# A two-layer decoder trunk: stick-breaking scores ahead of the V projection, dilated values behind the next q and k

## The chip, the core and the metric

One core of a Trainium2 chip runs the whole kernel. The metric is device time in microseconds of one execution. The engines are PE (matrix products), DVE (vector work), ACT (activation functions and copies), POOL (a second, slower vector engine) and SP (which issues most transfers). Each engine works through its own instructions strictly in order and waits on semaphores for the others.

## The reference

The input is x of 1 x 512 x 1024, with two layers of weights. A layer is a half-weighted SwiGLU, a hybrid mixer and another half-weighted SwiGLU. The mixer is:

```python
proj = h @ w_in
q_d, k_d = rope(...), rope(...)              # 12 dilated heads in 3 groups
o_dil = sum over groups of softmax-denominator weight * dilated_window_attention
# stick-breaking, 4 heads:
log_keep = where(past, log_sigmoid(-z), 0)
after = reverse_cumsum(log_keep) - log_keep
w = where(past, exp(log_sigmoid(z) + after), 0);  o_sb = w @ v
y = sigmoid(gate_dil) * (o_dil @ w_proj_dil) + sigmoid(gate_sb) * (o_sb @ w_proj_sb)
return y @ w_out
```

All is in float32.

## The kernel before, in words

Activations lie transposed, as eight tiles of 128 features x 512 tokens. Each float32 operand is split into a high and a low part in a rounded format (fp32r), and each product is made of three matmuls: high x high, low x high, high x low (`mm3`, lines 142 to 144; `project` chains eight of these, 24 matmuls, into one PSUM bank). Weights come in one long stream from DRAM, packed in the order of use by `_pack_layer`; ACT makes their high part `whi` (line 76) and DVE the low part `wlo` (line 77), two quarters of a chunk ahead.

PSUM has eight banks in four tags of two: m, t, s and o. A new tile of a tag waits until whoever reads the old one is done.

The mixer works in stages. First the **V projection** in two halves of 512 columns, token-major: half 0 in banks m, m, t, t and half 1 in s, s, o, o, with 32 x 3 matmuls each (lines 328 to 330). After the first of eight k steps of half 0, `norm.finish()` makes the root mean square: `rt`, one number per token on partitions (line 212), and `rb`, the same broadcast over a tile (matmuls at line 215, ACT copy at line 218). The V halves are then split into high and low by `split_v`: ACT scales by `rt` into the high part (line 338), DVE subtracts (line 339). Half 0 gives v0 (dilated heads without regrouping) and vs (stick heads); half 1 gives v12, in 16 pieces of 32 partitions x 512, since it is regrouped by residue of the token.

Then, for each of two head pairs, `qk_pair("plain")` projects q and k into m banks and splits them (DVE reads them with `rb` at line 377), and `stick(p, qk)` computes two heads. For each head and each of four query tiles, with 128, 256, 384 and 512 keys, PE makes a score block in an s bank (lines 400, 401 and the mask at 435), ACT takes abs, exp and ln, DVE a max-add (line 442), a running sum (443) and a subtraction that frees the s bank (445), and ACT the final exp (446). The weights are then transposed on PE (line 455), split (409, 410), and multiplied by vs (459).

Then, for s = 0 and 1, the dilated heads: `dil_scores` projects three rope pairs of q and k (lines 372 to 375) and makes scores, `dil_softmax` the softmax over the groups, and `dil_values` the transposes (572, 589) and the products with v0 (581) and v12 (599). `split_o` gives od0 and od1 (`od1h` is written by ACT at line 422). Gate projections, which depend on nothing but the normed input, fill PE between these steps: the table `GATES` says which pair of gates is projected at which place. Last, gates are applied (line 638 on), y is formed, and the output projection adds into x.

The code is written in this order, and a scheduler with a model of the engines then interleaves it: each engine's order is fixed when the kernel is built.

Of the kernel before, what the change touches and what calls it, by code (L numbers as in the profile page):

```python
# [15 lines left out]
P = 128  # L16
# [89 lines left out]
def trunk(ctx, tc, xin, win, gains, rope, masks, out, depth):  # L106
# [14 lines left out]
    def bank(tag):  # L121
        return psum.tile([P, 512], F32, name="ps_" + tag, tag=tag)
# [12 lines left out]

    ident = const.tile([P, P], F32, name="ident")
    make_identity(nc, ident)
    ones = const.tile([P, P], F32, name="ones")
    nc.vector.memset(ones, 1.0)

    def mm3(ps, w, v, start, stop):
# [15 lines left out]
    class Norm:  # L157


        def __init__(self, g, table=None):  # L160
            self.g = g * KD
            self.table = table
            last = table is None
            self.last = last
            self.h = [None] * KD
            self.acc = None
            self.rest = []

# [108 lines left out]
    def mixer(norm, nxt):  # L277
# [38 lines left out]
        nc.scalar.dma_start(sr, rope[1])  # L316


        pv = []
        for half in range(2):  # L320
            pv.append([bank(b) for b in ("mmtt", "ssoo")[half]])
            for k in range(KD):
                wh, wl = weights.quarter()
                for j in range(NT):
                    c = slice(j * P, (j + 1) * P)
                    ps = pv[half][j]
                    a, b = h[k][0][:, c], h[k][1][:, c]
                    nc.tensor.matmul(ps, a, wh, start=k == 0, stop=False)
                    nc.tensor.matmul(ps, a, wl, start=False, stop=False)
                    nc.tensor.matmul(ps, b, wh, start=False, stop=k == KD - 1)  # L330
                if half == 0 and k == 0:
                    norm.finish()
                    nc.gpsimd.tensor_mul(cr, cr, norm.rb)
                    nc.gpsimd.tensor_mul(sr, sr, norm.rb)

            def split_v(dst, src, sc):
                v = src.rearrange("p (h d) -> p h d", d=HD)
                nc.scalar.activation(dst[:, :, 0, :], v, AF.Copy, bias=0.0, scale=sc)
                nc.vector.scalar_tensor_tensor(dst[:, :, 1, :], v, sc, dst[:, :, 0, :].bitcast(F32),
                                               ALU.mult, ALU.subtract)  # L340

            if half == 0:
                v0, vs = [], []
                for j in range(NT):
                    sc = norm.rt[:, j:j + 1]
                    for lst, nm, off in ((v0, "v0", 0), (vs, "vs", 256)):
                        t = vp.tile([P, 4, 2, HD], F32R, name=f"{nm}_{j}", tag=f"{nm}_{j}")
                        split_v(t, pv[0][j][:, off:off + 256], sc)
                        lst.append(t)
            else:  # L350
                v12 = vp.tile([P, 4, 8, 2, HD], F32R, name="v12", tag="v12")
                for j in range(NT):
                    for r in range(4):
                        src = slice(32 * r, 32 * r + 32)
                        split_v(v12[32 * j:32 * j + 32, r], pv[1][j][src], norm.rt[src, j:j + 1])

        def to_t(ap):
            return ap.rearrange("p (j m r) -> p j r m", j=NT, m=32, r=4)
# [4 lines left out]
        def qk_pair(kind, view_q, view_k):  # L363

            res = []
            for which in ("q", "k"):
                ps = bank("m")
                project(ps, h)
                a = work("qa")
                if kind == "rope":  # L370
                    b = work("qb")
                    nc.vector.tensor_mul(a, ps, cr)
                    nc.vector.stream_shuffle(b, ps, ROT)
                    nc.gpsimd.tensor_mul(b, b, sr)
                    nc.gpsimd.tensor_add(a, a, b)
                else:
                    nc.vector.scalar_tensor_tensor(a, ps, SC if which == "q" else 1.0, norm.rb,
                                                   ALU.mult, ALU.mult)
# [38 lines left out]
            nc.vector.tensor_add(of[own], po[0:64], of[own])  # L417

        def split_o(of, nm):
            hi = mp.tile([P, T], F32R, name=nm + "h", tag=nm + "h")  # L420
            lo = mp.tile([P, T], F32R, name=nm + "l", tag=nm + "l")
            nc.scalar.copy(hi, of)
            nc.vector.tensor_sub(lo, of, hi.bitcast(F32))
            return hi, lo

        def stick(p, qk):
            of = work("of")
            for e in range(2):
                hd = 2 * p + e
                ws = []  # L430
                for j in range(NT):
                    w = (j + 1) * P
                    z = bank("s")
                    scores(z[:, :w], qk[e], tile_c(j), slice(0, w), True, False)
                    nc.tensor.matmul(z[:, j * P:w], identr, msbr, start=False, stop=True, skip_group_check=True)
                    a = pp.tile([P, T], F32, name="sw", tag="pp")
                    c = wk.tile([P, T], F32, name="sc", tag="sc", bufs=2)
                    av, cv, zv = a[:, :w], c[:, :w], z[:, :w]
                    nc.scalar.activation(av, zv, AF.Abs, bias=0.0, scale=1.0)
                    nc.scalar.activation(av, av, AF.Exp, bias=0.0, scale=-1.0)  # L440
                    nc.scalar.activation(av, av, AF.Ln, bias=1.0, scale=1.0)
                    nc.vector.scalar_tensor_tensor(av, zv, 0.0, av, ALU.max, ALU.add)
                    nc.vector.tensor_tensor_scan(cv[:, ::-1], av[:, ::-1], ones[:, 0:1].to_broadcast([P, w]), 0.0,  # L443
                                                 ALU.add, ALU.mult)
                    nc.vector.tensor_sub(cv, zv, cv)
                    nc.scalar.activation(av.rearrange("p (j r m) -> p j m r", r=4, m=32),
                                         cv.rearrange("p (j m r) -> p j m r", r=4, m=32),
                                         AF.Exp, bias=0.0, scale=1.0)
                    ws.append(a)
                po = bank("o")  # L450
                for i in range(NT):
                    n = NT - i
# [11 lines left out]
        def gate(d, b):  # L464
# [3 lines left out]
            if 0 <= i < KD:  # L468
                g = xpool.tile([P, T], F32, name="gate", tag=f"x{i}")
            else:  # L470
                g = mp.tile([P, T], F32, name="gate", tag="gate", bufs=6)
            nc.vector.tensor_mul(g, ps, norm.rb)
            return g

# [3 lines left out]
            for d in GATES[s, g]:  # L478
                gates[d] = (gate(d, 0), gate(d, 1))

        def dil_scores(s, st_a, st_b, pn, pm):

            qk0 = qk_pair("rope", same, same)
            fill(s, 0)
            for e in range(2):
                for i in range(2):
# [124 lines left out]

        last_exp = [None]
        os_ = []
        qs0 = qk_pair("plain", same, to_t)
        os_.append(stick(0, qs0))
        qs1 = qk_pair("plain", same, to_t)
        os_.append(stick(1, qs1))
        od = []
        for s in range(2):
            tl = dil_tiles()  # L620
            dil_scores(s, *tl)
            dil_softmax(*tl)
            od.append(dil_values(s, tl[2], tl[3]))
            fill(s, 3)
        st.close()

        st = ExitStack()
# [108 lines left out]
def _pack_layer(a, l):  # L736
# [25 lines left out]
    mix = [kmajor([(v, 256), (vs, 256)]), kmajor([(v + 256, 512)])]  # L762
    for p in range(2):
        mix += [blk(qs + P * p), blk(ks + P * p)]
    for s in range(2):
        for g in range(4):
            if g < 3:
# [51 lines left out]
```

## Time and profile before

| | us |
|---|---|
| median of three runs | 2175.48 |
| their range | 2173.88 to 2178.55 |
| the profiled execution's own time | 2173.67 |
| its span in the trace | 2171.8 |
| PE busy | 2140.2 (99%) |
| DVE busy | 1190.5 (55%) |
| ACT busy | 890.4 (41%) |
| first mixer, V projection | 374.35 to about 419 |

The first mixer lies at about 372 to 728 us of the span. A row of a windows view gives the window, its length, then busy time and number of instructions of PE, PE's weight loads, DVE, ACT and POOL, then the granted PE clock (1.00 is full), the share of DMA and GB/s. A matmul's listed duration (0.39 us for 512 columns) overlaps the next one; the distance between starts (0.23 us) is what it takes. A row of a waits view reads "engine and line of the waiting instruction <- what ended the wait: us in total, times, the longest".

### The profile page before, as it was taken

To read this page: it belongs to the slowest core of one execution; us is meant where nothing else is said; L and a number is where in the kernel's file an instruction comes from. 1 tells how busy PE (TensorE), PEld (TensorE's weight loads), DVE (VectorE), ACT (ScalarE), POOL (GpSimd) and SP (SyncE) were. 2 spreads that over 40 slices of the span, in tenths; PEclk is the share of its full clock that TensorE was granted. 3 is DMA by queue.
4 is the path that set the end of the run, shared out by engine and by line. 5 is a ranking of instruction groups with operands and counts; after the bars stand their busy time and mean duration, and the time that the engine had idled before them with its cause. 6 is when DMAs were issued, how large, how long until landed. Compare 5 with 4: busy or idle time off the path is not lost.

```text
span 2171.8 us, 25973 instructions
## 1 busy us (share of the span) xinstructions
PE 2140.2 (99%) x9828; PEld 1766.4 (81%) x9828; DVE 1190.5 (55%) x1892; ACT 890.4 (41%) x1572; POOL 369.4 (17%) x392
## 2 busy tenths in 40 slices
PE   8999999999999999999999999999999999999998
PEld 7888888878887888888888888888788788888887
DVE  5444433589867544443344444336897765444433
ACT  5333323566464433333333333236564543333332
POOL 2222100021312122210022220000223212222100
PEclk9999999999999999999999999999999999999999
DMA  4333334232224333333233333333222243323322
GB/s 152 97 97 97 95 111 126 88 93 82 81 76 128 96 97 98 97 97 94 91 97 97 97 97 102 108 121 93 87 83 78 78 127 96 97 97 97 97 92 84
DMA packets 64622, 212.81 MB, mean 98 GB/s; under 512 B 7408, under 2 KB 9456, under 8 KB 64496
## 3 DMA queue, kind: packets, MB, share of 16 engines
q1 hardware_dynamic: 63920, 210.10, 31.0%
q8 instruction: 77, 1.26, 0.2%
q10 hardware_dynamic: 576, 1.05, 0.2%
q14 instruction: 49, 0.40, 0.1%
HBM read 200.63 MB, written 6.29 MB: 95 GB/s over the span
## 4 chain that ended last, share of the span: by engine, by line
PE 92%; DVE 4%; issue 1%; ACT 1%; POOL 1%; DMA 0%; SPq 0%; DVEq 0%; POOLq 0%; ACTq 0%
PE ps_o L142 14%; PE ps_o L143 14%; PE ps_o L144 14%; PE ps_m L142 9%; PE ps_m L143 9%; PE ps_m L144 9%; PE ps_t L142 5%; PE ps_t L143 5%; PE ps_t L144 5%; DVE wlo L77 1%; DVE sc L443 1%; PE ps_o L599 0%; PE ps_s L401 0%; PE ps_s L400 0%; DVE pt L560 0%
## 5 line engine op out<-in xcount | busy, mean ns | idle before, releaser
L77 DVE TENSOR_TENSOR wlo<-wraw,whi 128x512 fp32r<-128x512 f32 x736 | 597.7, 815 | 614.5 <-ACT whi L76 613.9
L76 ACT CAST whi<-wraw 128x512 fp32r<-128x512 f32 x736 | 454.4, 621 | 959.0 <-PE ps_o L143 488.1
L142 PE MATMUL ps_m<-xh,whi 128*128 128x512 f32 x992 | 390.7, 394 | 9.9 <-ACT whi L76 6.4
L144 PE MATMUL ps_m<-xh,wlo 128*128 128x512 f32 x992 | 390.3, 393 | 0.5 <-DVE wlo L77 0.5
L143 PE MATMUL ps_m<-xl,whi 128*128 128x512 f32 x992 | 390.3, 393 | 0.0
L142 PE MATMUL ps_o<-fh,whi 128*128 128x512 f32 (+1 forms) x748 | 285.8, 382 | 0.0
L143 PE MATMUL ps_o<-fl,whi 128*128 128x512 f32 (+1 forms) x748 | 285.7, 382 | 0.0
L144 PE MATMUL ps_o<-fh,wlo 128*128 128x512 f32 (+1 forms) x748 | 285.7, 382 | 0.0
L239 POOL TENSOR_TENSOR fg<-fg,fs 128x512 f32<-128x512 f32 x88 | 114.9, 1307 | 928.1 <-ACT fs L238 928.1
L142 PEld LDWEIGHTS ps_m<-xh,whi 128*128 128x128 f32 x992 | 187.3, 189 | 51.0 <-ACT whi L76 8.2
L144 PEld LDWEIGHTS ps_m<-xh,wlo 128*128 128x128 f32 x992 | 187.2, 189 | 39.8 <-DVE wlo L77 2.4
L143 PEld LDWEIGHTS ps_m<-xl,whi 128*128 128x128 f32 x992 | 187.4, 189 | 37.9 <-DVE xl L180 0.8
L142 PE MATMUL ps_t<-xh,whi 128*128 128x512 f32 x480 | 187.2, 390 | 0.0
L144 PE MATMUL ps_t<-xh,wlo 128*128 128x512 f32 x480 | 187.0, 390 | 0.0
L143 PE MATMUL ps_t<-xl,whi 128*128 128x512 f32 x480 | 187.0, 390 | 0.0
L142 PE MATMUL ps_o<-xh,whi 128*128 128x512 f32 x448 | 174.4, 389 | 0.0
L143 PE MATMUL ps_o<-xl,whi 128*128 128x512 f32 x448 | 174.4, 389 | 0.0
L144 PE MATMUL ps_o<-xh,wlo 128*128 128x512 f32 x448 | 174.4, 389 | 0.0
L142 PEld LDWEIGHTS ps_o<-fh,whi 128*128 128x128 f32 x748 | 140.5, 188 | 30.1
L144 PEld LDWEIGHTS ps_o<-fh,wlo 128*128 128x128 f32 x748 | 140.5, 188 | 30.1
L143 PEld LDWEIGHTS ps_o<-fl,whi 128*128 128x128 f32 x748 | 140.5, 188 | 30.0
L240 POOL TENSOR_TENSOR fg<-fg,rb 128x512 f32<-128x512 f32 x88 | 114.9, 1307 | 6.3
(205 smaller groups left out, 2684.5 us busy)
## 6 DMA issues: line engine op xcount, KB each, us to landing
wraw<-in_w_dram SPq DMA_DIRECT2D x367, 512.0 KB, 3.5
spill<-x SPq DMA_DIRECT2D x16, 256.0 KB, 2.1
kh<-kh SPq DMA_DIRECT2D x32, 128.0 KB, 3.0
x<-spill SPq DMA_DIRECT2D x16, 256.0 KB, 3.4
x<-in_x_dram SPq DMA_DIRECT2D x8, 256.0 KB, 5.5
out_dram<-o SPq DMA_DIRECT2D x8, 256.0 KB, 2.9
wraw<-in_w_dram SPq DMA_DIRECT2D x2, 256.0 KB, 4.2
cr<-in_rope_dram ACTq DMA_DIRECT2D x2, 256.0 KB, 2.8
```

The source lines that it names most:

```text
L76: nc.scalar.copy(hi, src)
L77: nc.vector.tensor_sub(lo, src, hi.bitcast(F32))
L142: nc.tensor.matmul(ps, w[0], v[0], start=start, stop=False, skip_group_check=True)
L143: nc.tensor.matmul(ps, w[0], v[1], start=False, stop=False, skip_group_check=True)
L144: nc.tensor.matmul(ps, w[1], v[0], start=False, stop=stop, skip_group_check=True)
L239: nc.gpsimd.tensor_mul(g, g, s)
L240: nc.gpsimd.tensor_mul(g, g, norm.rb)
L443: nc.vector.tensor_tensor_scan(cv[:, ::-1], av[:, ::-1], ones[:, 0:1].to_broadcast([P, w]), 0.0, ALU.add, ALU.mult)
```

## The change

The mixer's order is rewritten. q and k of both stick pairs come first, each with its scores (`stick_scores`, the first half of the former `stick`); `norm.finish()` moves behind the first q projection. Then come V's two halves (`project_v`), half 0 now in banks t, t, o, o and half 1 in m, m, t, t. Then `stick_values` for both pairs. `dil_values(0)` is held back until the q and k of s = 1 have been projected. Gates 2 and 3 are both projected at place (1, 0), and gate 7 joins 4, 5 and 6 at (1, 3). To make room, the score tiles of a head share buffers (`half`, `full`), `ones` shrinks, vs lies in another pool, and od0 and od1 reuse its buffers. The weights are packed in the new order. All products stay the same.

```diff
-GATES = {(0, 0): (), (0, 1): (0, 1), (0, 2): (), (0, 3): (2,), (1, 0): (3,), (1, 1): (), (1, 2): (), (1, 3): (4, 5, 6)}
+GATES = {(0, 0): (), (0, 1): (0, 1), (0, 2): (), (0, 3): (), (1, 0): (2, 3), (1, 1): (), (1, 2): (), (1, 3): (4, 5, 6, 7)}
+OTAGS = {"os0": ("os0h", "os0l"), "os1": ("os1h", "os1l"), "od0": ("vs_0", "vs_1"), "od1": ("vs_2", "vs_3")}
...
-        pp = pool(st, "mixp", 8)
+        pp = pool(st, "mixp", 10)
...
-            pv.append([bank(b) for b in ("mmtt", "ssoo")[half]])
+        def project_v(half):
+            pv = [bank(b) for b in ("ttoo", "mmtt")[half]]
...
-                if half == 0 and k == 0:
-                    norm.finish()
...
                 ps = bank("m")
                 project(ps, h)
+                if norm.rb is None:
+                    norm.finish()
...
-        qs0 = qk_pair("plain", same, to_t)
-        os_.append(stick(0, qs0))
-        qs1 = qk_pair("plain", same, to_t)
-        os_.append(stick(1, qs1))
+        sw = []
+        for p in range(2):
+            sw.append(stick_scores(qk_pair("plain", same, to_t)))
+        for half in range(2):
+            project_v(half)
+        for p in range(2):
+            os_.append(stick_values(p, sw[p]))
         od = []
+        held = None
         for s in range(2):
+            qk0 = qk_pair("rope", same, same)
+            if held:
+                od.append(dil_values(0, *held))
             tl = dil_tiles()
-            dil_scores(s, *tl)
+            dil_scores(s, qk0, *tl)
             dil_softmax(*tl)
-            od.append(dil_values(s, tl[2], tl[3]))
-            fill(s, 3)
+            held = tl[2], tl[3]
+        od.append(dil_values(1, *held))
+        fill(1, 3)
```

**First place: DVE behind the end of V's second half (layer 1).** A row reads: line, operation, what is written <- what is read, shape; the number behind a name tells buffers apart. Before, the splits of V's second half (v12, from the s and o banks) mix with weight splits:

```order
L339 SCALAR_TENSOR_TENSOR v12_3190<-ps_o_3053,rt_2889,v12_3190 32x8x64
L77 TENSOR_TENSOR wlo_3243<-wraw_3224,whi_3242 128x512
L339 SCALAR_TENSOR_TENSOR v12_3190<-ps_s_3051,rt_2889,v12_3190 32x8x64
L339 SCALAR_TENSOR_TENSOR v12_3190<-ps_o_3052,rt_2889,v12_3190 32x8x64
L339 SCALAR_TENSOR_TENSOR v12_3190<-ps_s_3050,rt_2889,v12_3190 32x8x64
L339 SCALAR_TENSOR_TENSOR v12_3190<-ps_o_3053,rt_2889,v12_3190 32x8x64
L77 TENSOR_TENSOR wlo_3270<-wraw_3267,whi_3269 128x512
L339 SCALAR_TENSOR_TENSOR v12_3190<-ps_s_3051,rt_2889,v12_3190 32x8x64
L377 SCALAR_TENSOR_TENSOR qa_3258<-ps_m_3223,rb_2904 128x512
L339 SCALAR_TENSOR_TENSOR v12_3190<-ps_o_3052,rt_2889,v12_3190 32x8x64
L339 SCALAR_TENSOR_TENSOR v12_3190<-ps_s_3050,rt_2889,v12_3190 32x8x64
```

After, they come from the m and t banks and mix with steps of the second stick pair, heads 2 and 3 (lines 447, 448 and 450 are the former 442, 443 and 445; 330 is the former 339, 81 the former 77). Nine rows stand between the first split and the rows below, the first split among them: five splits, head 2's last max-add, running sum and subtraction, each 128x512, and one weight split (wlo). Then comes head 3:

```order
L330 SCALAR_TENSOR_TENSOR v12_2861<-ps_m_3430,rt_2903,v12_2861 32x8x64
L330 SCALAR_TENSOR_TENSOR v12_2861<-ps_t_3431,rt_2903,v12_2861 32x8x64
L330 SCALAR_TENSOR_TENSOR v12_2861<-ps_t_3432,rt_2903,v12_2861 32x8x64
L447 SCALAR_TENSOR_TENSOR sw_3215<-ps_s_3217,sw_3215 128x128
L330 SCALAR_TENSOR_TENSOR v12_2861<-ps_m_3429,rt_2903,v12_2861 32x8x64
L330 SCALAR_TENSOR_TENSOR v12_2861<-ps_m_3430,rt_2903,v12_2861 32x8x64
L448 SCALAR_TENSOR_TENSOR sc_3221<-sw_3215,ones_109 128x128
L330 SCALAR_TENSOR_TENSOR v12_2861<-ps_t_3431,rt_2903,v12_2861 32x8x64
L330 SCALAR_TENSOR_TENSOR v12_2861<-ps_t_3432,rt_2903,v12_2861 32x8x64
L450 TENSOR_TENSOR sc_3221<-ps_s_3217,sc_3221 128x128
L447 SCALAR_TENSOR_TENSOR sw_3164<-ps_s_3229,sw_3164 128x256
L330 SCALAR_TENSOR_TENSOR v12_2861<-ps_m_3429,rt_2903,v12_2861 32x8x64
```

The last row is the fourth split of ps_m_3429, the one after which that bank is free; it is the thirteenth of the sixteen. The steps of heads 2 and 3 stand between the splits now, and no qa.

**Second place: PE at the end of V's second half (layer 1).** Before, V's last matmuls, into an o bank, are followed by the projection of the first stick q into an m bank:

```order
L330 MATMUL ps_o_3052<-whi_3140,xl7_2801 128x512
L328 MATMUL ps_o_3053<-whi_3140,xh7_2800 128x512
L329 MATMUL ps_o_3053<-wlo_3141,xh7_2800 128x512
L330 MATMUL ps_o_3053<-whi_3140,xl7_2801 128x512
L142 MATMUL ps_m_3223<-xh0_2086,whi_3158 128x512
L143 MATMUL ps_m_3223<-xl0_2087,whi_3158 128x512
L144 MATMUL ps_m_3223<-xh0_2086,wlo_3159 128x512
L142 MATMUL ps_m_3223<-xh1_2186,whi_3158 128x512
L143 MATMUL ps_m_3223<-xl1_2187,whi_3158 128x512
```

After, V's last matmuls go into a t bank, and score blocks of head 3 with 128, 256 and 384 keys follow (lines 402, 403 and 440 are the former 400, 401 and 435), then the first rope q projection into the m bank that ps_m_3429 had (line 146 is the former 142):

```order
L341 MATMUL ps_t_3432<-wlo_3520,xh7_2800 128x512
L342 MATMUL ps_t_3432<-whi_3519,xl7_2801 128x512
L402 MATMUL ps_s_3217<-kh_3160,qh_3116 128x128
L403 MATMUL ps_s_3217<-kl_2839,qh_3116 128x128
L440 MATMUL ps_s_3217<-msbr_150,identr_149 128x128
L402 MATMUL ps_s_3229<-kh_3160,qh_3116 128x256
L403 MATMUL ps_s_3229<-kl_2839,qh_3116 128x256
L440 MATMUL ps_s_3229<-msbr_150,identr_149 128x128
L402 MATMUL ps_s_3241<-kh_3160,qh_3116 128x384
L403 MATMUL ps_s_3241<-kl_2839,qh_3116 128x384
L440 MATMUL ps_s_3241<-msbr_150,identr_149 128x128
L146 MATMUL ps_m_3775<-xh0_2086,whi_3537 128x512
```

Projections that stood behind V now stand ahead of it, and a short run of score blocks separates V from the next projection.

**Third place: PE at the norm's broadcast (layer 1).** Before, the matmuls that broadcast rt (line 215) stand among V's:

```order
L330 MATMUL ps_t_2863<-whi_2926,xl4_2496 128x512
L328 MATMUL ps_t_2864<-whi_2926,xh4_2495 128x512
L329 MATMUL ps_t_2864<-wlo_2927,xh4_2495 128x512
L215 MATMUL ps_s_2899<-ident_104,rt_2889 128x128 x4
L330 MATMUL ps_t_2864<-whi_2926,xl4_2496 128x512
L328 MATMUL ps_m_2861<-whi_2942,xh5_2596 128x512
L329 MATMUL ps_m_2861<-wlo_2943,xh5_2596 128x512
```

After, they stand (line 220) between the projection of k of the first pair (ps_m_2930) and that of q of the second (ps_m_3076):

```order
L148 MATMUL ps_m_2930<-xh6_2701,wlo_2882 128x512
L146 MATMUL ps_m_2930<-xh7_2800,whi_2881 128x512
L147 MATMUL ps_m_2930<-xl7_2801,whi_2881 128x512
L148 MATMUL ps_m_2930<-xh7_2800,wlo_2882 128x512
L220 MATMUL ps_s_2913<-ident_104,rt_2903 128x128 x4
L146 MATMUL ps_m_3076<-xh0_2086,whi_2933 128x512
L147 MATMUL ps_m_3076<-xl0_2087,whi_2933 128x512
```

The broadcast moved from the middle of V to the border between two m-bank projections; the sum of squares (line 208 of the changed kernel) stands 14 matmuls ahead of it.

More of the change, by code (lines that the diff above doesn't have):

```diff
@@ L137, in trunk @@
     make_identity(nc, ident)
-    ones = const.tile([P, P], F32, name="ones")
+    ones = const.tile([P, 1], F32, name="ones")
     nc.vector.memset(ones, 1.0)
@@ L316, in mixer, with split_v @@
         nc.scalar.dma_start(sr, rope[1])
-        pv = []
-        for half in range(2):
-            pv.append([bank(b) for b in ("mmtt", "ssoo")[half]])
+        v0, vs = [], []
+        v12 = vp.tile([P, 4, 8, 2, HD], F32R, name="v12", tag="v12")
+        def split_v(dst, src, sc):
+            v = src.rearrange("p (h d) -> p h d", d=HD)
+            nc.scalar.activation(dst[:, :, 0, :], v, AF.Copy, bias=0.0, scale=sc)
+            nc.vector.scalar_tensor_tensor(dst[:, :, 1, :], v, sc, dst[:, :, 0, :].bitcast(F32),
+                                           ALU.mult, ALU.subtract)
+        def project_v(half):
+            pv = [bank(b) for b in ("ttoo", "mmtt")[half]]
             for k in range(KD):
@@ L325, in mixer @@
                     c = slice(j * P, (j + 1) * P)
-                    ps = pv[half][j]
                     a, b = h[k][0][:, c], h[k][1][:, c]
-                    nc.tensor.matmul(ps, a, wh, start=k == 0, stop=False)
-                    nc.tensor.matmul(ps, a, wl, start=False, stop=False)
-                    nc.tensor.matmul(ps, b, wh, start=False, stop=k == KD - 1)
-                if half == 0 and k == 0:
-                    norm.finish()
[L333 to L344, printed above, removed]
+                    nc.tensor.matmul(pv[j], a, wh, start=k == 0, stop=False)
+                    nc.tensor.matmul(pv[j], a, wl, start=False, stop=False)
+                    nc.tensor.matmul(pv[j], b, wh, start=False, stop=k == KD - 1)
+            for j in range(NT):
+                if half == 0:
                     sc = norm.rt[:, j:j + 1]
-                    for lst, nm, off in ((v0, "v0", 0), (vs, "vs", 256)):
-                        t = vp.tile([P, 4, 2, HD], F32R, name=f"{nm}_{j}", tag=f"{nm}_{j}")
-                        split_v(t, pv[0][j][:, off:off + 256], sc)
+                    for lst, nm, off, pl in ((v0, "v0", 0, vp), (vs, "vs", 256, mp)):
+                        t = pl.tile([P, 4, 2, HD], F32R, name=f"{nm}_{j}", tag=f"{nm}_{j}")
+                        split_v(t, pv[j][:, off:off + 256], sc)
                         lst.append(t)
-            else:
-                v12 = vp.tile([P, 4, 8, 2, HD], F32R, name="v12", tag="v12")
-                for j in range(NT):
+                else:
                     for r in range(4):
                         src = slice(32 * r, 32 * r + 32)
-                        split_v(v12[32 * j:32 * j + 32, r], pv[1][j][src], norm.rt[src, j:j + 1])
+                        split_v(v12[32 * j:32 * j + 32, r], pv[j][src], norm.rt[src, j:j + 1])
         def to_t(ap):
@@ L368, in qk_pair @@
                 project(ps, h)
+                if norm.rb is None:
+                    norm.finish()
+                    nc.gpsimd.tensor_mul(cr, cr, norm.rb)
+                    nc.gpsimd.tensor_mul(sr, sr, norm.rb)
                 a = work("qa")
@@ L424, in split_o, with stick_scores @@
             return hi, lo
-        def stick(p, qk):
-            of = work("of")
+        def stick_scores(qk):
+            half = pp.tile([P, T], F32, name="sw", tag="pp")
+            heads = []
             for e in range(2):
-                hd = 2 * p + e
+                full = [pp.tile([P, T], F32, name="sw", tag="pp") for _ in range(2)]
                 ws = []
@@ L449, in stick, with stick_values @@
                     ws.append(a)
+                heads.append(ws)
+            return heads
+        def stick_values(p, heads):
+            of = work("of")
+            for e, ws in enumerate(heads):
+                hd = 2 * p + e
                 po = bank("o")
@@ L470, in gate @@
             else:
-                g = mp.tile([P, T], F32, name="gate", tag="gate", bufs=6)
+                g = mp.tile([P, T], F32, name="gate", tag="gate", bufs=8)
             nc.vector.tensor_mul(g, ps, norm.rb)
```

28 lines of the change are left out of this document (15 added, 13 removed).

## The prediction

> **What bounds the kernel now.** I read the page first, then the stretches of the first mixer with their idle time, then the waits of PE, then the groups of one shape for durations. The page's engine line and the chain:
>
> ```profile
> PE 2140.2 (99%) x9828; PEld 1766.4 (81%) x9828; DVE 1190.5 (55%) x1892; ACT 890.4 (41%) x1572; POOL 369.4 (17%) x392
> PE 92%; DVE 4%; issue 1%; ACT 1%; POOL 1%; DMA 0%; SPq 0%; DVEq 0%; POOLq 0%; ACTq 0%
> ```
>
> TensorE (PE) is the bound. The change adds and removes no matmul, so it can only change how long PE waits, and how fast it runs. The stretches of the first mixer show where PE waits today; PE's busy time is the second number after the window's length.
>
> ```profile
> core 0: us, PE busy (x) PEld busy (x) DVE busy (x) ACT busy (x) POOL busy (x), PEclk, DMA share, GB/s
> 372.00:420.00 48.00, 48.00 (x221) 39.92 (x220) 19.81 (x35) 18.42 (x33) 5.07 (x6) 1.00 0.36 113
> 420.00:440.00 20.00, 20.00 (x89) 16.30 (x88) 19.24 (x27) 16.67 (x25) 0.00 (x0) 1.00 0.22 65
> 460.00:482.00 22.00, 17.38 (x87) 13.58 (x86) 18.90 (x29) 11.91 (x27) 6.11 (x4) 1.00 0.28 78
> 560.00:604.00 44.00, 42.45 (x228) 35.10 (x227) 37.27 (x84) 17.91 (x36) 19.12 (x38) 1.00 0.26 72
> 649.00:654.00 5.00, 3.70 (x18) 2.27 (x17) 2.11 (x4) 1.82 (x3) 0.00 (x0) 1.00 0.00 0
> ```
>
> 372 to 420 is the V projection: PE never waits. 420 to 440 holds the split of V's second half on DVE and ACT: both are nearly full, and PE, which has query and key projections to do, still never waits. PE waits at the end of the first stick pair (22.00 - 17.38 = 4.62 us), in the dilated values of s = 0 (1.55) and at the end of the dilated values of s = 1 (1.30). PE's waits in those places, summed over both layers:
>
> ```profile
> PE ps_s L400 <- DVE sc L445: 3.9, 4, 1.3
> PE ps_t L142 <- ACT od1h L422: 2.6, 2, 1.3
> PE ps_m L142 <- DVE gate L472: 2.5, 2, 1.2
> ```
>
> The second layer repeats them, with one thing more:
>
> ```profile
> 1535.00:1557.00 22.00, 17.65 (x82) 13.79 (x81) 18.88 (x29) 12.45 (x28) 5.40 (x4) 0.95 0.30 84
> 1550.00:1554.80 4.80, 2.94 (x19) 2.24 (x17) 3.90 (x8) 2.96 (x7) 0.00 (x0) 1.00 0.13 51
> 1554.80:1558.20 3.40, 2.98 (x7) 2.41 (x8) 3.34 (x7) 3.13 (x8) 0.26 (x1) 0.50 0.50 96
> ```
>
> After a stretch in which PE was busy 2.94 of 4.80 us, the granted clock is 0.50 for 3.4 us. Two pairs of neighbouring matmuls inside it and behind it give the price:
>
> ```profile
> 1556.66 0.63 PE L142 MATMUL ps_m<-xh,whi 128*128 128x512 f32 x1
> 1557.09 0.63 PE L143 MATMUL ps_m<-xl,whi 128*128 128x512 f32 x1
> 1558.54 0.40 PE L144 MATMUL ps_m<-xh,wlo 128*128 128x512 f32 x1
> 1558.77 0.39 PE L142 MATMUL ps_m<-xh,whi 128*128 128x512 f32 x1
> ```
>
> 0.43 us from start to start against 0.23. Seven matmuls there lost 7 x 0.20 = 1.4 us. So the same stall cost 4.62 us in layer 1 and 4.35 + 1.4 = 5.75 in layer 2.
>
> **What the change gives back.** The scores of both stick pairs now run among the projections of the second pair and of V, so the DVE crowd at 460 to 482 is spread out: -4.6 in layer 1, -5.75 in layer 2. Held back, the first dilated values come behind the next q and k: I take half of the 1.55, -0.8 (an estimate between 0 and -1.55). At od1, 21 projection matmuls now stand between the last v12 matmul and the first that needs od1h, where three stood: at 0.23 us that is 4.8 us of cover against a wait of 1.30: -1.3. Gate 7's two projections leave the tail for this; there the output projection's first 21 matmuls need only y0 to y6, so I cost that at nothing (up to 1 us if that cover fails, counted below). Sum: -6.7 in layer 1, -7.85 in layer 2.
>
> **What it takes: V's second half.** This is the large term. V is now projected last, its second half into banks m, m, t, t, and what PE does next (second place in the order above) are three score blocks and then the q projection of the dilated heads, which needs the first of those m banks. On DVE (first place) 13 of the 16 splits of V, head 2's last step and head 3's first ones stand ahead of the release of that bank. The durations of V's splits, and of the shapes between them:
>
> ```profile
> L338 ACT ACTIVATE v<-ps_s,rt x8: 679/682/683, 417.9 to 429.0; 32x512 fp32r<-32x512 f32 x8
> L339 DVE SCALAR_TENSOR_TENSOR v<-ps_s,rt,v x8: 737/744/756, 418.6 to 431.6; 32x512 fp32r<-32x512 f32 x8
> L339 DVE SCALAR_TENSOR_TENSOR v<-ps_o,rt,v x8: 742/748/759, 420.2 to 436.1; 32x512 fp32r<-32x512 f32 x8
> ```
>
> ```profile
> L77 DVE TENSOR_TENSOR wlo<-wraw,whi 128x512 fp32r<-128x512 f32 x108 | 86.5, 807 | 47.7 <-ACT whi L76 47.5
> L443 DVE TENSOR_TENSOR_SCAN sc<-sw,ones 128x512 f32<-128x512 f32 x4 | 8.1, 2034 | 0.0
> L442 DVE SCALAR_TENSOR_TENSOR sw<-ps_s,sw 128x512 f32<-128x512 f32 x4 | 2.7, 680 | 0.0
> L445 DVE TENSOR_TENSOR sc<-ps_s,sc 128x512 f32<-128x512 f32 x4 | 2.7, 674 | 0.0
> L443 DVE TENSOR_TENSOR_SCAN sc<-sw,ones 128x128 f32<-128x128 f32 x4 | 2.4, 604 | 0.1
> L442 DVE SCALAR_TENSOR_TENSOR sw<-ps_s,sw 128x256 f32<-128x256 f32 x4 | 1.7, 417 | 0.0
> L445 DVE TENSOR_TENSOR sc<-ps_s,sc 128x128 f32<-128x128 f32 x4 | 1.1, 280 | 0.0
> L442 DVE SCALAR_TENSOR_TENSOR sw<-ps_s,sw 128x128 f32<-128x128 f32 x4 | 1.1, 279 | 0.0
> ```
>
> From the first split to the one that frees the bank: 13 x 0.747 = 9.7; head 2's 512-wide step 0.68 + 2.03 + 0.67; one wlo 0.81; head 3's 128-wide step 0.28 + 0.60 + 0.28; the start of the 256-wide step 0.42. The second group is 5.8, together 15.5 us. ACT makes the high part of each split in 0.68 and keeps ahead. DVE's first split began at 418.6 and V's last three matmuls were issued from
>
> ```profile
> 418.40 0.39 PE L328 MATMUL ps_o<-whi,xh 128*128 128x512 f32 x1
> ```
>
> on, 0.23 apart, to 419.1: DVE has a start of 0.5 us. PE has three score blocks in between: 128, 256 and 384 columns, twice each, and three masks of 128, 2 x 768 + 384 = 1920 columns at 0.23 / 512 each, about 0.9 us. Idle: 15.5 - 0.5 - 0.9 = 14.1; I take 14.0. PE meets it as two waits for a score bank (each for DVE's subtraction, about 5.9 and 7.9 us) and a rest of under 1 us for the m bank. Bounds: 8.6, if all of that but the splits were done earlier or lay under PE's work (9.7 - 1.1), and 15.5, if nothing overlaps.
>
> **The clock behind that wait.** 14 us of waiting with under 1 us of work in them is more than the 1.86 us in 4.80 that brought the clock to 0.50 in layer 2. I take +1.4 per layer once, with bounds of 0 (layer 1's 4.62 us of waits cost nothing, its row reads 1.00) and 2.8 (a drop in each of two places). The Trainium skill, TensorE: Matmul & The Clock Gate, section "What's actually happening", has a rule that speaks against this change: after one idle window of about 3.4 us the array gets half of its clock pulses, until it has been busy for about as long. By that rule the first matmuls after such a wait would lose about half of 3.4, 1.7 us as an estimate from that page; layer 2's rows, 3.4 us at 0.50, agree with it.
>
> **The first q and k.** Before, the norm's broadcast (rb) was made among V's matmuls, which don't need it (third place). Now q's and k's banks are the two m banks, and q1's projection must wait until DVE has read q0's with rb.
>
> ```profile
> 382.07 0.95 PE L203 MATMUL ps_s<-ones,acc 128*128 128x1 f32 x8
> 384.09 0.16 DVE L212 SCALAR_TENSOR_TENSOR rt<-ra,r 128x4 f32<-128x4 f32 x1
> L218 ACT COPY rb<-ps_s 128x512 f32<-128x512 f32 x1 | 0.6, 587 | 2.7 <-PE ps_s L215 2.7
> L377 DVE SCALAR_TENSOR_TENSOR qa<-ps_m,rb 128x512 f32<-128x512 f32 x4 | 2.8, 690 | 0.1
> ```
>
> rt is there 2.2 us after the sum of squares began, and in the changed order 14 matmuls (14 x 0.23 = 3.2 us) stand between the two: in time. Then 0.59 + 0.69 and the hand-overs, about 1.5 us, in PE's path (bounds 0.7 and 2.0).
>
> **Smaller waits.** PE changes kind more often (scores between V's matmuls), heads 1 and 2 may wait for a score bank, and the last k's DMA lands just ahead of the dilated scores. No row shows these in the new places; the nearest are the score waits above, 1.3 us at the longest. I take +1.0 per layer, bounds 0 and 3.0 (two such waits and the tail).
>
> **The sum.** Layer 1: 14.0 + 1.4 + 1.5 + 1.0 - 6.7 = +11.2. Layer 2: 14.0 + 1.4 + 1.5 + 1.0 - 7.85 = +10.05. Together +21.2. The profiled execution took 2173.67 us (its span is 2171.8), the median of the runs 2175.48, 0.1% more. 2173.67 + 21.2 = 2194.9; forecast 2195.
>
> **The rivals.**
>
> *Faster: the split stays hidden.* One mechanism: V's banks come free as fast as PE needs them. The row 420 to 440 speaks for it: 16 splits, PE at 20.00 of 20.00. But there PE had q and k projections for free m banks, 89 matmuls of cover; now nothing but 0.9 us of scores. The gains then stand against 1.5 + 1.0: -4.2 and -5.35, 2164. It decides where wait and clock together stay below 4.2 us per layer. Chance 0.11.
>
> *Half the wait.* DVE is through with head 2's 512-wide step when V ends, or PE reaches that place later than DVE does: the wait is 7 to 9 us. With 8.0: +5.2 and +4.05, 2183 (2179 to 2187). For it: the bound 8.6. Against it: the order of DVE is fixed and has the scan of 2.03 between the splits. Chance 0.20. Between this and the rival before lies no change, 2169.3 to 2178: 0.07, where gains and wait cancel.
>
> *The clock does not fall.* 2195 - 2.8 = 2192; layer 1's row of 1.00 speaks for it, layer 2's 0.50 against. It lies inside the forecast's own range. That the change does not do what it says (that the V projection is put back ahead of the scores in the program's order) is excluded by the rows in the order; I give it nothing.
>
> **How the numbers follow.** Forecast 0.62, with its own range of 2187 to 2207: the upper end is 15.5 + 2.8 + 2.0 + 3.0 - 6.7 = 16.6 in layer 1 and 15.45 in layer 2, together 32, or 2206. Range: from 2179, the lower end of the half wait, to 2207; it leaves out the faster rival and no change, 0.18, and little above. About 0.2% (4.35 us) is what a measurement of this kernel can tell from no change: faster 0.11, same 0.07, slower 0.62 + 0.20 = 0.82.
>
> **What would show it.** In the profile after: no wait in the first pair's last head (the 4.62 gone); no wait of PE for od1h; behind V's last matmul PE idle 12 to 15 us per layer, put down to DVE's score subtraction (line 450 of the changed kernel) and to a split of V (its line 330); a granted clock below 1.00 right after; PE idle about 1.5 us behind the broadcast of rb. I am wrong if PE works on through V's split, or if a third place waits as long as that one.

## The result and the profile after

The changed kernel takes 2186.43 us (2186.26 to 2186.89, 4 runs) against 2174.78 for the kernel before (4 runs): ratio 1.0053, 95% interval 1.0041 to 1.0065, 11.65 us slower. The forecast was 2195, range 2179 to 2207: direction and main cause right, the size nearly twice too large. The two profiled executions are 13.2 us apart (2186.89 and 2173.67), their spans 13.3 (2185.1 and 2171.8); what follows accounts for these.

The page of the changed kernel: PE's work is the same, the span is longer.

```profile
span 2185.1 us, 26025 instructions
PE 2140.3 (98%) x9828; PEld 1771.1 (81%) x9828; DVE 1184.3 (54%) x1892; ACT 892.5 (41%) x1572; POOL 371.5 (17%) x392
```

The stretches of its first mixer; V's projection ends at 448.8:

```profile
core 0: us, PE busy (x) PEld busy (x) DVE busy (x) ACT busy (x) POOL busy (x), PEclk, DMA share, GB/s
372.00:390.00 18.00, 16.60 (x82) 13.76 (x81) 8.68 (x17) 7.77 (x14) 4.00 (x6) 1.00 0.43 142
446.00:464.00 18.00, 6.05 (x24) 4.88 (x24) 17.27 (x27) 17.26 (x30) 0.00 (x0) 0.69 0.13 42
464.00:487.00 23.00, 23.00 (x109) 19.12 (x109) 20.00 (x29) 13.41 (x25) 6.26 (x4) 0.95 0.14 47
560.00:604.00 44.00, 44.00 (x244) 38.03 (x243) 34.47 (x84) 21.93 (x50) 15.20 (x34) 1.00 0.25 78
```

One stretch stands out: 446 to 464 has PE at 6.05 of 18 us, with DVE and ACT nearly full and the clock below 1. Layer 2 has the same stretch, with nearly the same numbers, at 1527 to 1545:

```profile
1527.00:1545.00 18.00, 6.05 (x24) 4.91 (x23) 17.27 (x27) 17.26 (x30) 0.00 (x0) 0.72 0.15 46
```

The stretches with waits of before are clean (560 to 604 has 44.00 of 44.00). PE's largest wait, both layers together, and a selection of PE's rows behind V's end in layer 1 (start, listed duration; in brackets the idle time and its releaser):

```profile
PE ps_s L402 <- DVE sc L450: 23.7, 4, 7.1
```

```profile
448.54 0.40 PE L342 MATMUL ps_t<-whi,xl 128*128 128x512 f32 x1
448.95 0.28 PE L440 MATMUL ps_s<-msbr,identr 128*128 128x128 f32 x1
453.94 0.55 PE L402 MATMUL ps_s<-kh,qh 128*128 128x256 f32 x1 [4.71 <-DVE sc L450]
461.95 0.69 PE L402 MATMUL ps_s<-kh,qh 128*128 128x384 f32 x1 [7.14 <-DVE sc L450]
463.16 0.77 PE L146 MATMUL ps_m<-xh,whi 128*128 128x512 f32 x1
465.86 0.63 PE L146 MATMUL ps_m<-xh,whi 128*128 128x512 f32 x1
466.28 0.50 PE L147 MATMUL ps_m<-xl,whi 128*128 128x512 f32 x1
```

These are V's last matmul, rows of three score blocks with two long waits between them, then the q projection, whose first matmuls are 0.43 us apart instead of 0.23. On DVE, a selection of what PE waited for, from V's first split to the step that released the second score bank, and the split behind it that frees the m bank:

```profile
448.17 0.73 DVE L330 SCALAR_TENSOR_TENSOR v<-ps_m,rt,v 32x512 fp32r<-32x512 f32 x1
450.30 1.23 DVE L448 TENSOR_TENSOR_SCAN sc<-sw,ones 128x512 f32<-128x512 f32 x1
453.10 0.69 DVE L450 TENSOR_TENSOR sc<-ps_s,sc 128x512 f32<-128x512 f32 x1
...
461.60 0.29 DVE L450 TENSOR_TENSOR sc<-ps_s,sc 128x128 f32<-128x128 f32 x1
462.26 1.54 DVE L330 SCALAR_TENSOR_TENSOR v<-ps_m,rt,v 32x512 fp32r<-32x512 f32 x2
```

**An account from start to start.** A matmul of 512 columns is listed with 0.39 us but takes 0.23 in a full row, so idle time in a listing is too small by up to 0.16 for each wait. Two rows of the kernel before show it:

```profile
464.25 0.39 PE L142 MATMUL ps_m<-xh,whi 128*128 128x512 f32 x1
465.96 0.36 PE L400 MATMUL ps_s<-kh,qh 128*128 128x256 f32 x1 [1.32 <-DVE sc L445]
```

The starts are 1.71 apart, so 1.48 us were lost, not 1.32. So I took, for each PE matmul of the mixer, the distance to the next start less 0.2275, 0.171, 0.114 or 0.061 us (512, 384, 256, and 128 or fewer columns), and added up, place by place, what is left where it exceeds 0.12. Layer 1, in us (both kernels have 1636 matmuls there):

| place | before | after |
|---|---|---|
| behind the norm's broadcast | 0 | 1.62 |
| behind V's end: waits | 0 | 13.4 |
| matmuls at half clock after it | 0 | 1.5 |
| end of the first stick pair (464 to 482) | 5.54 | 0 |
| first dilated values (580 to 604) | 2.94 | 0 |
| a gate (627) | 0.64 | 0 |
| od1 (650) | 1.80 | 0 |
| others | 0.13 | 2.14 |
| all that are at most 0.12 over | 18.4 | 17.8 |
| sum | 29.4 | 36.4 |

The mixer took 345.0 us before and 352.0 after, and 346.0 and 352.3 in layer 2: +7.0 and +6.3.

### The profile page after: what moved, and what is told of

It is laid out like the page before. It is cut to its first block, busy times and chain, and to the rows that moved or that the text cites. A ratio compares the mean times of both kernels' runs of the same rounds, so it can differ in the third digit from the quotient of the medians.

```text
span 2185.1 us, 26025 instructions
## 1 busy us (share of the span) xinstructions
PE 2140.3 (98%) x9828; PEld 1771.1 (81%) x9828; DVE 1184.3 (54%) x1892; ACT 892.5 (41%) x1572; POOL 371.5 (17%) x392
## 4 chain that ended last, share of the span: by engine, by line
PE 96%; DVE 2%; ACT 1%; DMA 0%; POOL 0%; issue 0%; SPq 0%; DVEq 0%; ACTq 0%; POOLq 0%
PE ps_o L146 14%; PE ps_o L147 14%; PE ps_o L148 14%; PE ps_m L146 11%; PE ps_m L147 11%; PE ps_m L148 10%; PE ps_t L146 5%; PE ps_t L148 5%; PE ps_t L147 5%; PE ps_s L402 1%; PE ps_s L403 1%; PE ps_o L610 1%; PE ps_t L341 1%; PE ps_t L342 1%; PE ps_t L340 1%; DVE v L330 0%
```

## The experiments

The theory: PE waits behind V because the banks that it needs next (first for scores, then for the projection) are released in DVE's order behind V's splits; cure either the bank or the amount of work, and the wait goes. The rival: DVE has too much work in that stretch in all, and the wait moves on. A second question is which part of the change brought the gains. There are three sets of four kernels; the kernel before took 2173.95, 2174.59 and 2175.05 us beside them. A ratio is always to the kernel before of the same set.

**1. V's halves in the other order** (banks by position).

```diff
-        for half in range(2):
+        for half in (1, 0):
             project_v(half)
```

> The half of V with 16 small splits is projected first, the other half last; banks stay by position (t, t, o, o, then m, m, t, t). Theory (PE waits for banks that DVE frees in order behind V's splits): behind V's end stand 16 pieces of 0.48 us instead of 0.75, and fewer of them ahead of the m bank; PE waits about 5 us there in place of 13.4 and the clock stays up: 2186.4 - 2 x (14.9 - 5) = 2166.6 us, between 2162 and 2171. Rival (DVE has too much work in all, wherever the banks are): the wait moves, 2180 us or more.

2177.54 us (2174.94 to 2178.39), ratio 1.0016 [1.0007, 1.0026]. Faster than the changed kernel by 8.9 us, less than the theory's 19.8. Most of the wait moved to where the next half takes over the t banks (layer 1; behind V's end 1.7 us are left, in layer 2 4.2):

```profile
429.00:440.00 11.00, 6.92 (x24) 5.26 (x23) 9.16 (x14) 9.43 (x15) 0.00 (x0) 0.84 0.11 42
446.00:464.00 18.00, 16.50 (x81) 13.71 (x80) 14.38 (x29) 14.05 (x32) 0.00 (x0) 1.00 0.27 87
```

```profile
PE ps_t L340 <- DVE v L330: 4.1, 1, 4.1
```

The splits delay whichever matmul needs their bank next; here that was V's own second half. I had only thought of the m banks.

**2. V's banks**, the half with 16 splits in o and t.

```diff
-            pv = [bank(b) for b in ("ttoo", "mmtt")[half]]
+            pv = [bank(b) for b in ("mmtt", "oott")[half]]
```

> Only the banks of V are changed: first half in m, m, t, t, second half in o, o, t, t, so that both m banks are free at V's end. Theory (the bank, not the work, makes PE wait): the q projection follows V at once, 48 matmuls of cover for the splits; 13 to 14.9 us per layer go: 2186.4 - 2 x 13.9 = 2158.6 us, between 2156 and 2164, faster than before. Rival (too much DVE work in that stretch): PE waits as long a little later, 2183 to 2187 us.

2170.22 us (2169.51 to 2170.82), ratio 0.9982 [0.9973, 0.9991]: 16 us faster than the changed kernel and faster than before, by changing one string. The choice of banks is shown to make the wait. The string also changes PE's order: in the changed kernel PE met the wait at score blocks, which stood ahead of the projection; here, with its bank free, the projection starts straight behind V's last matmul and the first score block comes ten matmuls later.

```profile
448.58 0.39 PE L342 MATMUL ps_t<-whi,xl 128*128 128x512 f32 x1
448.81 0.39 PE L146 MATMUL ps_m<-xh,whi 128*128 128x512 f32 x1
451.08 0.23 PE L402 MATMUL ps_s<-kh,qh 128*128 128x128 f32 x1
```

But the theory's 2158.6 was missed: of the 27.8 us that it expected, 11.6 did not come, and waits stand 17 and 26 us behind V's end (the row of waits counts layer 1).

```profile
448.00:464.00 16.00, 16.00 (x75) 13.33 (x74) 15.40 (x23) 15.45 (x27) 2.92 (x2) 1.00 0.19 67
464.00:480.00 16.00, 12.01 (x51) 9.14 (x50) 15.53 (x23) 9.28 (x18) 5.59 (x4) 0.93 0.26 82
```

```profile
PE ps_m L146 <- DVE qb L375: 3.8, 2, 2.2
```

DVE is busy 15.4 and 15.5 of 16 us: 16 splits, head 3's steps and the weight splits are more than PE's cover there. Now the m banks are late because their readers (qa, qb) stand in the same queue. Theory and rival are each half right.

**3. V ahead of the scores again**, in its former banks and with the norm's broadcast among its matmuls, all else as changed (the banks, the broadcast and the packing are left out here).

```diff
+        for half in range(2):
+            project_v(half)
         for p in range(2):
             sw.append(stick_scores(qk_pair("plain", same, to_t)))
-        for half in range(2):
-            project_v(half)
```

> V is projected first again, in its former banks, with the norm's broadcast among its matmuls; scores of both pairs, then values, dilated values held back and gate 7 early stay as changed. Theory: neither the wait behind V (14.9 us with the clock) nor that for the broadcast (1.6) is there; of the 11 us of waits per layer that went, those at the end of the first pair may come back (5.5 us): between 2174.8 - 2 x 9.5 = 2155.8 and 2167 us. Rival (the gains hang on V standing behind the scores): 2172 to 2176 us.

2180.13 us (2178.28 to 2184.04), ratio 1.003 [1.002, 1.004]. My expectation fell, and so did the rival's. The wait at the end of the first pair is back, and a second one stands at the second pair; the stretch of the first dilated values has none:

```profile
460.00:482.00 22.00, 17.49 (x87) 13.70 (x87) 18.88 (x29) 11.92 (x28) 6.11 (x4) 1.00 0.25 79
518.00:532.00 14.00, 9.39 (x40) 6.73 (x39) 11.98 (x29) 10.94 (x22) 1.92 (x2) 0.88 0.31 95
560.00:604.00 44.00, 44.00 (x244) 37.99 (x243) 33.66 (x83) 20.54 (x49) 19.59 (x40) 1.00 0.22 70
```

So the gain at 464 to 482 belongs to V standing behind the scores, as the forecast had it.

**4. The tail alone on the kernel before**: dilated values held back, gates as changed.

> The kernel before with the tail parts alone: first dilated values held back behind the next q and k, gates as changed, vs and od sharing buffers. Theory: the waits in the first dilated values (about 2.9 us per layer, start to start) and at od1 (1.5) and one for a gate (0.5) go, about 0.8 come at the gates: 2174.8 - 2 x 4 = 2166.8 us, between 2164 and 2170. Rival (these waits went because the scores stand elsewhere): 2173 to 2177 us.

2177.25 us (2174.01 to 2179.65), ratio 1.0014 [1.0005, 1.0023]: slower, where I expected 7 us faster. The largest loss is at 520 to 532, first the kernel before, then this one:

```profile
520.00:532.00 12.00, 12.00 (x65) 10.27 (x64) 11.85 (x24) 7.88 (x15) 2.91 (x2) 1.00 0.24 66
```

```profile
520.00:532.00 12.00, 9.67 (x43) 7.65 (x42) 11.18 (x24) 6.34 (x12) 2.90 (x2) 0.86 0.23 66
```

**5. Fewer splits in the changed kernel.** Its banks stay; V's second half is split in 8 full-height pieces and regrouped by DMA.

```diff
-                        split_v(v12[32 * j:32 * j + 32, r], pv[j][src], norm.rt[src, j:j + 1])
+                    for g in range(2):
+                        t = xpool.tile([P, 4, 2, HD], F32R, name="vt", tag=f"x{2 * j + g}")
+                        split_v(t, pv[j][:, 256 * g:256 * g + 256], norm.rt[:, j:j + 1])
+                        for r in range(4):
+                            nc.sync.dma_start(v12[32 * j:32 * j + 32, r, 4 * g:4 * g + 4].bitcast(F32),
+                                              t[32 * r:32 * r + 32].bitcast(F32))
```

> The changed kernel, its banks as they are, but V's second half is split in 8 pieces of 128x256 (about 0.48 us on each of DVE and ACT) into the free x tiles and regrouped by 32 small DMAs, in place of 16 pieces of 0.75. Theory (PE waits for what stands in DVE's order ahead of the release of the m bank): 4 pieces and head 2's step, 1.9 + 1.9 = 3.8 us, stand there in place of 14.9; the clock stays up: 2186.4 - 2 x 11 = 2164 us, between 2161 and 2170. Rival (the DMAs on SP's queue hold up the weights, or PE waits for something else there): 2178 us or more.

2170.99 us (2168.42 to 2171.55), ratio 0.998 [0.9971, 0.9989]; 1 us over the theory's upper end (five small waits, 2.9 us together, stand at 472 to 478). The wait behind V is one of 2.45 us, with the clock at 1.00:

```profile
449.28 0.27 PE L443 MATMUL ps_s<-msbr,identr 128*128 128x128 f32 x1
452.00 0.47 PE L146 MATMUL ps_m<-xh,whi 128*128 128x512 f32 x1 [2.45 <-DVE vt L330]
452.31 0.40 PE L147 MATMUL ps_m<-xl,whi 128*128 128x512 f32 x1
```

Here the bank is the same and the work is less; in run 2 the work is the same and the bank another. Each alone takes 15 to 16 us off. So the wait is shown from both sides to come from what stands ahead of a bank's release.

**6. The second pair's q and k into o banks**, on top of run 2.

```diff
-                ps = bank("m")
+                ps = bank("o" if kind == "plain" and pairs[0] == 1 else "m")
```

> The variant with V's second half in o, o, t, t, and the second stick pair's q and k projected into o banks. Theory: the wait of 1.6 us per layer behind the norm's broadcast, put down to the m bank of q0, goes: 2170.2 - 2 x 1.6 = 2167.0 us. Rival: PE waits for the broadcast's readers all the same, 2170 us.

2166.90 us (2166.42 to 2167.23), ratio 0.9965 [0.9953, 0.9978]; 2167.0 was expected. The wait behind the broadcast (16.60 of 18 us in the changed kernel) is gone:

```profile
372.00:390.00 18.00, 18.00 (x84) 14.96 (x83) 6.75 (x14) 6.94 (x11) 2.08 (x4) 1.00 0.44 138
```

**7 and 8. Other banks and regrouping by DMA together**, with run 6's edit and without it.

> The last variant with V's second half regrouped by DMA as well. Theory: both remaining waits of the variant with other banks go, those behind V (1.8 + 2.4 and smaller, with 1.5 of half clock: 6 us per layer, from a DVE that is busy 15.5 of 16 us) and the 1.6: 2170.2 - 2 x 7.6 = 2155 us, between 2153 and 2160. Rival (DVE's crowd stays, since the steps of the stick heads fill it): 2165 us or more.

> V's second half in o, o, t, t, regrouped by DMA; second pair's q and k in m banks. Theory: only the 6 us per layer behind V go: 2170.2 - 12 = 2158 us, between 2156 and 2164. Rival (DVE's crowd stays): 2168 us or more.

With it 2164.44 us (2163.98 to 2164.57), ratio 0.9956 [0.9941, 0.9971]; without it 2168.04 (2165.14 to 2168.37), 0.9967 [0.9954, 0.998]. The first is 10 us faster than before and the fastest of all. Both stay 9 to 10 us above the theory, at the rival's mark. Behind V PE no longer waits, but about 20 us later it does; the faster of the two (windows of layer 1, the wait summed over both layers):

```profile
446.00:464.00 18.00, 18.00 (x90) 15.09 (x90) 15.77 (x32) 13.52 (x32) 3.62 (x3) 1.00 0.38 92
464.00:482.00 18.00, 15.62 (x73) 12.50 (x72) 16.27 (x32) 15.80 (x30) 4.96 (x4) 0.81 0.44 133
```

```profile
PE ps_o L474 <- ACT pth L414: 4.5, 4, 1.3
```

PE has caught up with the first pair's values, and ACT and DVE, at 15.8 and 16.3 of 18, set the pace; the clock falls too. This fits the rival: the stick heads' own work fills DVE and ACT. No run took any of that work away.

**9 and 10. The old tail** (dilated values and gates in their former places; the line of `GATES` is left out) under the changed order, and under the fastest variant.

```diff
-        held = None
...
-            qk0 = qk_pair("rope", same, same)
-            if held:
-                od.append(dil_values(0, *held))
             tl = dil_tiles()
-            dil_scores(s, qk0, *tl)
+            dil_scores(s, qk_pair("rope", same, same), *tl)
             dil_softmax(*tl)
-            held = tl[2], tl[3]
-        od.append(dil_values(1, *held))
-        fill(1, 3)
+            od.append(dil_values(s, tl[2], tl[3]))
+            fill(s, 3)
```

> The changed kernel with its order of scores and V, but dilated values and gates in their former places. Theory (each wait that went is a gain of the part that moved it): the waits in the first dilated values (2.9 us per layer), at od1 (1.5) and at a gate (0.5) come back, 0.8 goes: 2186.4 + 2 x 4.1 = 2194.6 us, between 2191 and 2197. Rival (as in the kernel before with the tail parts alone, these parts bring nothing by themselves): 2183 to 2189 us.

> The fastest variant so far (other banks, regrouped by DMA) with dilated values and gates in their former places. Theory as for the run before: 2164.4 + 8.2 = 2172.6 us, between 2169 and 2175. Rival: 2162 to 2167 us.

2188.22 us (2187.29 to 2189.62), ratio 1.006 [1.0045, 1.0075], and 2165.18 (2164.57 to 2166.33), 0.9954 [0.994, 0.9969]: 1.8 and 0.7 us over the same kernels with the new tail, which is within the intervals, as the rival said. The wait at od1 is back (8.70 of 10), but the first dilated values run almost without a wait even though the program doesn't hold them back (run 9):

```profile
560.00:604.00 44.00, 43.88 (x242) 37.58 (x241) 34.35 (x87) 23.11 (x54) 19.66 (x38) 1.00 0.28 84
654.00:664.00 10.00, 8.70 (x44) 6.47 (x44) 6.00 (x9) 2.72 (x5) 1.81 (x2) 1.00 0.00 0
```

So that gain doesn't need the hold in the program. Nor does it need V behind the scores, since run 3 has none of these waits either.

**11 and 12. The hold alone, and the gates alone**, on the kernel before.

> The kernel before with the first dilated values held back, and nothing else. Together with the gates this made it 3 us slower (2177.25 against 2173.95). Theory (gate 2, taken from its place behind the first dilated values, was cover for a crowded DVE, and the hold is worth its wait): 2174.6 - 2 x 2.9 = 2168.8 us, between 2167 and 2173. Rival (the hold itself crowds DVE where the next q and k are made): 2176 to 2180 us.

> The kernel before with the gates' new places, and nothing else. Theory (cover is lost where gate 2 stood): 2176 to 2181 us. Rival (the hold did it; the gates save the wait at od1, 1.5 us per layer, less 0.8): 2171 to 2174 us.

The hold: 2173.50 us (2172.11 to 2178.12), ratio 0.9995 [0.9986, 1.0005], no difference; 560 to 604 has 42.46 of 44 as before (42.45). Neither expectation met it. The traces say why: in run 11, PE, ACT and POOL run the same operations on the same tiles in the same order as in the kernel before, and so does DVE but for the size of one memset. In the kernel before, the scheduler had already put the next q and k ahead: DVE reads them at 537.1 and 544.5, and the first dilated values begin at 573.4. The hold asked for an order that was there, in run 9 too (553.5 and 558.5 against 577.9). In the same way run 4 has the order of run 12: its hold did nothing either, and all of its effect is the gates'.

The gates: 2177.35 (2174.41 to 2180.27), 1.0012 [1.0002, 1.0022], as expected. The wait at 520 to 532 is run 4's:

```profile
520.00:532.00 12.00, 9.66 (x53) 7.91 (x52) 11.15 (x24) 7.24 (x13) 2.92 (x2) 1.00 0.23 67
```

```profile
PE ps_m L145 <- DVE qb L376: 2.4, 2, 1.9
```

In run 9 and in the changed kernel, where V stands behind the scores, this doesn't happen (12.00 of 12.00). In the kernel before, the scheduler had put gate 2 here: the fifth and sixth gate projections, which are gate 2's, are read by DVE at 520.3 and 533.1. In run 12 they are read at 542.6 and 549.5, so the cover is gone, as the theory of run 12 had it. On the other side, run 12 has no wait at od1, and only 1.0 us (layer 2: 1.6) of the 2.9 in the first dilated values.

The two profiled executions with one order also differ: run 4's (2176.69 us) has the clock at 0.50 for 3.4 us inside this window, run 12's (2174.41 us) has 1.00, as the PEclk of 0.86 and 1.00 in the two rows says. So part of the loss in run 4's execution is the clock.

## Why the prediction was right, and where it was off

**V's second half: right.** Forecast 14.0 us of waiting per layer as two waits for a score bank of 5.9 and 7.9 and a rest; measured 13.4, as 4.9 and 7.4 (start to start) and 1.1 in small ones. Both long waits are for a score bank, as forecast; none is put down to a split itself, and at the m bank 0.35 is left. DVE's stretch to the last piece of the m bank was 14.9 us, not 15.5: the 512-wide running sum took 1.23 and not the 2.03 of the group's mean, which mixed 1.2 and 2.3 (last section). One bound doesn't follow from the sum: 9.7 less the 0.5 and 0.9 of the sum is 8.3, not 8.6. Runs 2 and 5 show the cause from both sides.

**The clock: right.** Forecast 1.4, measured 1.5 (in layer 2 ten matmuls and 2.1). Windows of the changed kernel, from the first wait to behind the last:

```profile
449.30:452.80 3.50, 0.00 (x0) 0.00 (x0) 3.37 (x5) 3.40 (x5) 0.00 (x0) 1.00 0.00 0
452.90:466.40 13.50, 5.23 (x14) 4.16 (x15) 12.84 (x21) 12.48 (x22) 0.00 (x0) 0.50 0.13 39
463.00:466.40 3.40, 3.30 (x9) 2.63 (x9) 3.24 (x6) 2.75 (x6) 0.00 (x0) 0.50 0.00 0
466.40:470.00 3.60, 3.60 (x19) 2.99 (x18) 2.14 (x4) 2.04 (x3) 0.00 (x0) 0.99 0.00 0
```

The clock fell inside the first wait, about 3.8 us after its start at 449.0, and was back at about 466.4, 3.3 us after the projection had begun at 463.16. The page TensorE: Matmul & The Clock Gate of the Trainium skill, section "What's actually happening", gives about 3.4 us of idling for the fall and about 3.4 us of work for the return; this trace agrees. The rows of layer 2 that the prediction set beside that rule agree with its length alone, since no idle stretch of 3.4 us stood ahead of them (2.94 of 4.80 busy). The rival "the clock does not fall" is excluded.

**The first q and k: right**, 1.5 and 1.62, and run 6 removes it by its bank alone.

**Smaller waits: right in size.** Forecast 1.0; measured 2.1 at three places (0.55 at a score, 0.75 at the gates, 0.84 in the output projection), less 0.6 in shorter distances.

**What the change gives back: this step failed**, at 6.7 us in layer 1 where 11.05 were gained. Its parts were too small. The end of the first pair gave 5.54, not 4.6, and od1 with its followers 1.80, not 1.3, because I took idle time from windows of busy time. Those two gains are tied to their parts: V ahead again brings the first back (run 3), the old gates the second (runs 9 and 10), and the new gates alone remove the second (run 12). The first dilated values gave all of their wait, 2.94 start to start, where I took half of a listed 1.55; the gate's 0.64 I had left out. And the reason I gave isn't borne out: I put the dilated gain down to the hold, yet the next q and k stood ahead of the first dilated values in the kernel before already (run 11), and run 9 has nearly all of the gain without the hold (0.5 us of waits are left). Which part brings it stays open: the new gates alone bring some 1.9 of the 2.9 (run 12), the new order nearly all of it with the old gates (run 9). With 11.05 in place of 6.7 (the five rows of the column before, with the 0.13 of others), my own sum is 14.0 + 1.4 + 1.5 + 1.0 - 11.05 = +6.9, against +7.0 measured.

The measured 2186.43 lies just below the forecast's own 2187 to 2207, where the prediction had put the rival "half the wait" (2179 to 2187). But that rival's mechanism, a wait of 7 to 9 us, is excluded by the 13.4: the number came down through the larger gains, not through a shorter wait.

The rival on the faster side would have needed the wait and clock under 4.2 us per layer; they were 14.9. With the true gains that limit was about 7.9 (11.05 - 1.6 - 1.5), still far off.

## What to carry to other kernels

When a stage is moved, ask which bank the bound engine needs next behind it, and count what stands ahead of that bank's release in the order of the engine that reads it: a change of bank letters was worth 16 us here. Count both costs and gains from start to start of the bound engine's instructions, not from busy time. Test a part alone only together with the order it relies on: the tail was worth at most 2 us under the new order, and cost 3.3 under the old one. And see whether an edit changed the built order before reading its time: the hold did not.

## What the runs showed of the hardware that I had not expected

The same running sum of 128x512 on DVE takes 1.20 to 1.23 us, or 2.30 to 2.31. In the kernel before, the five long ones of eight are those with a POOL tensor operation beside them; one of them, DVE and POOL:

```profile
462.78 2.30 DVE L443 TENSOR_TENSOR_SCAN sc<-sw,ones 128x512 f32<-128x512 f32 x1
```

```profile
462.39 1.61 POOL L375 TENSOR_TENSOR qa<-qa,qb 128x512 f32<-128x512 f32 x1
```

PE's wait behind 464.25, shown further up, is for the step that this scan belongs to. In the changed kernel no scan (running sum) of 512 columns has POOL beside it, and all eight take 1.20 to 1.23. It also goes the other way: in run 3 the scan at 486.06 takes 1.21, and the POOL operation beside it 2.73. The Trainium skill, SBUF — State Buffer, section "SBUF: two separate sides", says that a DVE operation with two SBUF inputs and a GpSimd operation that reads SBUF block each other; the rows agree with that, one of the two being 1.1 us longer each time. No run here took POOL's work away, so the cause is argued, not shown.

The half clock also came without any long wait: in layer 2 of the kernel before, after gaps of 1.2 and 1.4 us within 4.8 (PE busy 2.94). The same matmuls with the same gaps left it at 1.00 in layer 1:

```profile
476.44:481.24 4.80, 2.95 (x19) 2.25 (x17) 3.90 (x8) 2.96 (x7) 0.00 (x0) 1.00 0.14 57
```

So gaps of this size cost about 1.5 us more in one place and nothing in another, and the runs don't show what decides.
